# Counting argmax hits by sign masks on ScalarE for two of eight batches, in a gather and scatter kernel

## The chip, the cores and the metric

The kernel runs on one core of a Trainium2 chip. The metric is the device time of one execution in microseconds (us), lower is better. All runs quoted are with a granted TensorE clock of 1.0. TensorE, VectorE, ScalarE, GpSimd and SyncE appear in the profile as PE, DVE, ACT, POOL and SP; PEld is TensorE's weight load.

## The reference

```python
B, S, H = (8, 2048, 2560)          # scores [B,S,S], values [B,S,H], float32
best_j = np.argmax(scores, axis=2)
gathered = values[b_idx, best_j, :].copy()
out = np.zeros_like(values)
np.add.at(out, (b_idx, best_j, slice(None)), gathered)
```

A row j of a batch is thus written as `count[j] * values[j]`, where `count[j]` says how many rows of `scores` have their maximum in column j. About 37% of the counts are 0, 37% are 1 and 26% are higher.

## The kernel before

For each tile of 128 rows of scores, VectorE finds the maximum and then its column. After each four tiles, one-hot masks and a small matmul add up the counts:

```python
rows = room[:, place(x):place(x) + S]
nc.vector.max(out=mx[:], in_=rows)                                      # L196
nc.vector.max_index(out=am[:, g, :], in_max=mx[:], in_values=rows)      # L197
if g == G - 1:
    ...  # lo, hi, oh_lo, oh_hi on VectorE, then 4 matmuls into cnt_ps  # L200 to L212
```

`room` is one area of SBUF that holds the tiles of scores in a ring. The first two laps also use the places in which gathered rows will stand later (`NX` = 7 of them, besides `NB` = 14 permanent slots):

```python
def place(x):
    return NV * H + (x % turn - NX if x < 2 * turn else (x - 2 * turn) % NB) * S   # turn = NX + NB
```

When a batch is counted, GpSimd issues its output: rows with count 1 are copied from DRAM to DRAM (`copy_once`), rows with count 0 get zeros, and rows with higher counts are gathered into `room`, scaled on ScalarE and scattered. For batch 0 this part is:

```python
def gathers():
    for k in range(MCAP):                                   # MCAP = 5
        v = stage()
        gather(v, mi[:, k:k + 1])
        nc.scalar.activation(out=v, in_=v, func=Copy, bias=0.0, scale=mc[:, k:k + 1])   # L370, name of Copy cut short
        staged.append(v)
        ...
if b == 0:
    zeros(range(nz))                 # 7 transfers
    while tiles[0] < turn + NX:      # until all tiles in the gathers' places are read
        yield
    gathers()
...
for k in range(MCAP):
    scatter(staged[k], mi[:, k:k + 1], ...)
```

The order of the program is kept on TensorE, VectorE, ScalarE and SyncE. `yield` marks where the scan of the next batch's tiles goes on.

Of the kernel before, what the change touches and what calls it, by code (L numbers as in the profile page):

```python
# [8 lines left out]
FP32 = mybir.dt.float32  # L9
BF16 = mybir.dt.bfloat16  # L10
FP16 = mybir.dt.float16
INT32 = mybir.dt.int32
U32 = mybir.dt.uint32
ALU = mybir.AluOpType
P = 128
# [21 lines left out]
def kernel(  # L37
# [6 lines left out]
    nc = tc.nc  # L44
    B, S, S2 = scores.shape
    _, _, H = values.shape
    assert S == S2
    NT = S // P
    BIG = float(1 << 24)
    R = 4  # L50
    G = 4
    NV = 6
    NX = NV * H // S
    NB = 14
    NM = NT // 2
    NE = 16
    LE = P // NE
# [6 lines left out]
    out_flat = out.rearrange("b s h -> (b s) h")  # L64
    last_row = nc.gpsimd.to_reg(B * S - 1)

    consts = ctx.enter_context(tc.tile_pool(name="consts", bufs=1))
    small = ctx.enter_context(tc.tile_pool(name="small", bufs=3))
    fin = ctx.enter_context(tc.tile_pool(name="fin", bufs=2))
    ohp = ctx.enter_context(tc.tile_pool(name="ohp", bufs=1))  # L70
    lev = ctx.enter_context(tc.tile_pool(name="lev", bufs=1))
    psum_c = ctx.enter_context(tc.tile_pool(name="psum_c", bufs=2, space=bass.MemoryType.PSUM))
    psum_f = ctx.enter_context(tc.tile_pool(name="psum_f", bufs=1, space=bass.MemoryType.PSUM))
# [13 lines left out]
    row_f = consts.tile([P, NT], FP32)  # L87
# [3 lines left out]
    lane_f = consts.tile([P, P], FP32)  # L91
# [7 lines left out]
    ones = consts.tile([P, P], BF16)  # L99
# [15 lines left out]
    zero1 = consts.tile([P, 1], FP32)  # L115
    nc.vector.memset(zero1[:], 0.0)

    zrow = ctx.enter_context(nc.sbuf_tensor([P, H], FP32))
    nc.scalar.copy(zrow[:], zero1[:].to_broadcast([P, H]))


    room = ctx.enter_context(nc.sbuf_tensor([P, NV * H + NB * S], FP32))
    nc.scalar.copy(room[:, 0:NV * H - NX * S], zero1[:].to_broadcast([P, NV * H - NX * S]))
    turn = NX + NB
# [6 lines left out]
    loads, x = {}, 0  # L131
    while x < B * NT:
        n = 1
        most_n = 1 if x < 2 or 2 * turn - 6 <= x < 2 * turn else 2 if x < 4 or 2 * turn <= x < 4 * NT else R
        while n < most_n and (x + n) % NT and place(x + n) == place(x) + n * S:
            n += 1
        loads[x] = n
        x += n

    ones_i = ctx.enter_context(nc.sbuf_tensor([P, B * NT], INT32))  # L140
    zero_i = ctx.enter_context(nc.sbuf_tensor([P, B * NT], INT32))
    many_i = ctx.enter_context(nc.sbuf_tensor([P, B * NM], INT32))
    many_c = ctx.enter_context(nc.sbuf_tensor([P, B * NM], FP32))

# [5 lines left out]
    def after_waits(ins):  # L150
        tc.declare_no_dep(ins.ins, group="zrow", reason="GpSimd has waited for the transfers ahead of it")
# [12 lines left out]
    def gather(v, idx, note=lambda ins: None):  # L164
        note(nc.gpsimd.indirect_dma_start(  # L165
            out=v, out_offset=None, in_=values_flat[:, :],
            in_offset=bass.IndirectOffsetOnAxis(ap=idx, axis=0), bounds_check=B * S - 1, oob_is_err=False))
# [9 lines left out]
    def stage():  # L177
        v = room[:, vslot[0] * H:(vslot[0] + 1) * H]
        vslot[0] = (vslot[0] + 1) % NV
        return v  # L180

    def count_steps(b, cnt_ps):

        am = None
        for t in range(NT):
            x = b * NT + t
            if x in loads:
                n = loads[x]
                nc.sync.dma_start(out=room[:, place(x):place(x) + n * S],
                                  in_=scores[b, t * P:(t + n) * P, :].rearrange("(p r) s -> p (r s)", r=n))  # L190
            g = t % G
            if g == 0:
                am = small.tile([P, G, 8], U32, name="am")
            rows = room[:, place(x):place(x) + S]
            mx = small.tile([P, 8], FP32)
            nc.vector.max(out=mx[:], in_=rows)  # L196
            nc.vector.max_index(out=am[:, g, :], in_max=mx[:], in_values=rows)  # L197
            if g == G - 1:
                lo = small.tile([P, G], U32)
                nc.vector.tensor_single_scalar(out=lo[:], in_=am[:, :, 0], scalar=P - 1, op=ALU.bitwise_and)  # L200
                hi = small.tile([P, G], U32)
                nc.vector.tensor_single_scalar(out=hi[:], in_=am[:, :, 0], scalar=7, op=ALU.logical_shift_right)  # L202
                oh_lo = small.tile([P, G, P], BF16)
                nc.vector.tensor_tensor(  # L204
                    out=oh_lo[:], in0=lo[:].unsqueeze(2).to_broadcast([P, G, P]),
                    in1=lane_f[:].unsqueeze(1).to_broadcast([P, G, P]), op=ALU.is_equal)
                oh_hi = small.tile([P, G, NT], BF16)
                nc.vector.tensor_tensor(  # L208
                    out=oh_hi[:], in0=hi[:].unsqueeze(2).to_broadcast([P, G, NT]),
                    in1=lane_f[:, 0:NT].unsqueeze(1).to_broadcast([P, G, NT]), op=ALU.is_equal)  # L210
                for k in range(G):
                    nc.tensor.matmul(out=cnt_ps[:], lhsT=oh_lo[:, k, :], rhs=oh_hi[:, k, :],  # L212
                                     start=(t == G - 1 and k == 0), stop=(t == NT - 1 and k == G - 1))
            tiles[0] = x + 1
            yield

    def level_engines(rank):

# [59 lines left out]
    def value_steps(b, cnt_ps):  # L278

        cnt = fin.tile([P, NT], FP32)  # L280
# [23 lines left out]
        for c in range(2):  # L304
            nc.vector.tensor_tensor_scan(out=inc[:, c, :], data0=ones_f[:], data1=m[:, c, :], initial=0.0,
                                         op0=ALU.mult, op1=ALU.add)
# [15 lines left out]
        if b == B - 1:  # L322
            level_engines(rank[:, 0, :])
        hi = fin.tile([P, 2, NT], U32)
        nc.vector.tensor_copy(hi[:], rank[:])
        nc.vector.tensor_single_scalar(out=hi[:], in_=hi[:], scalar=7, op=ALU.logical_shift_right)
        lo = fin.tile([P, NT], U32)
# [4 lines left out]
            out=oh[:], in0=lo[:].unsqueeze(2).to_broadcast([P, NT, P]),  # L332
            in1=fill_f[:].unsqueeze(1).to_broadcast([P, NT, P]), op=ALU.is_equal)

        ez = fin.tile([P, NT, NT], FP16)
        nc.vector.tensor_tensor(  # L336
            out=ez[:], in0=hi[:, 0, :].unsqueeze(2).to_broadcast([P, NT, NT]),
            in1=lane_f[:, 0:NT].unsqueeze(1).to_broadcast([P, NT, NT]), op=ALU.is_equal)
        em = fin.tile([P, NT, NM], FP16)
        nc.vector.tensor_tensor(  # L340
            out=em[:], in0=hi[:, 1, :].unsqueeze(2).to_broadcast([P, NT, NM]),
            in1=lane_f[:, 0:NM].unsqueeze(1).to_broadcast([P, NT, NM]), op=ALU.is_equal)
        put = fin.tile([P, NT, 2 * NM + NT], FP16)
        nc.vector.tensor_tensor(out=put[:, :, 0:NM], in0=em[:], in1=row1_f[:].unsqueeze(2).to_broadcast([P, NT, NM]), op=ALU.mult)  # L344
        nc.vector.tensor_tensor(out=put[:, :, NM:2 * NM], in0=em[:], in1=cnt[:].unsqueeze(2).to_broadcast([P, NT, NM]), op=ALU.mult)
        nc.vector.tensor_tensor(out=put[:, :, 2 * NM:], in0=ez[:], in1=row1_f[:].unsqueeze(2).to_broadcast([P, NT, NT]), op=ALU.mult)  # L346
# [12 lines left out]
        for dst, x, n in ((zi, 2 * NM, NT), (mi, 0, NM)):  # L359
            nc.vector.scalar_tensor_tensor(out=dst, in0=e[:, x:x + n], scalar=float(b * S - 1), in1=l_ps[:, x:x + n],  # L360
                                           op0=ALU.add, op1=ALU.add)
# [40 lines left out]
    with tc.manual_schedule(engines={ET.PE, ET.DVE, ET.Activation, ET.SP}):  # L402
        pending = iter(())
        for b in range(B):
            cnt_ps = psum_c.tile([P, NT], FP32)
            for _ in count_steps(b, cnt_ps):
                next(pending, None)
            for _ in pending:
                pass
            pending = value_steps(b, cnt_ps)  # L410
            for _ in range((1, 4, 0)[min(b, 2)]):
                next(pending)
        for _ in pending:
            pass
        full = fin.tile([1, 2], FP32)
        nc.vector.tensor_reduce(out=full[:, 0:1], in_=tots[0:1, 0, 0:B - 1], op=ALU.max, axis=mybir.AxisListType.X)
        nc.vector.tensor_reduce(out=full[:, 1:2], in_=tots[0:1, 1, :], op=ALU.max, axis=mybir.AxisListType.X)
        over = fin.tile([1, 3], FP32)
        nc.vector.tensor_single_scalar(out=over[:, 0:1], in_=full[:, 0:1], scalar=float(ZCAP * P), op=ALU.is_gt)
        nc.vector.tensor_single_scalar(out=over[:, 1:2], in_=full[:, 1:2], scalar=float(MCAP * P), op=ALU.is_gt)  # L420
        nc.vector.tensor_single_scalar(out=over[:, 2:3], in_=most[0:1, :], scalar=float(ZLAST * LE), op=ALU.is_gt)
        over_i = fin.tile([1, 1], INT32)
        nc.vector.tensor_reduce(out=over_i[:], in_=over[:], op=ALU.max, axis=mybir.AxisListType.X)

    more = nc.values_load(over_i[0:1, 0:1], engines=[mybir.EngineType.Pool], min_val=0, max_val=2)
    spilt = tc.alloc_semaphore("spilt")
    with tc.If(more > 0):

# [3 lines left out]
        def one_by_one(ins):  # L432
            nonlocal n_spilt, last
            writes_out(ins)
            after_waits(ins)
            tc.add_to_no_dep_group("zrow", ins.ins)
            ins.then_inc(spilt, 16)
            tc.info.no_tile_sem_insts.add(ins.ins.name)
            n_spilt += 1
            with tc.issue_after(ins.ins):  # L440
                last = nc.gpsimd.wait_ge(spilt, 16 * n_spilt)
# [6 lines left out]
        for b in range(B):  # L448
            for k in range(MCAP, NM):
# [7 lines left out]
                with tc.issue_after(scaled.ins):  # L457
                    scatter(zrow[:], many_i[:, i:i + 1], one_by_one)

    last = nc.gpsimd.wait_ge(landed, 16 * n_free[0])  # L460
    with tc.issue_after(last.ins):
        nc.gpsimd.dma_reset()
# [30 lines left out]
```

## Time and profile before

| What | Before |
|---|---|
| Median of 4 runs beside the changed kernel | 828.87 us (827.58 to 828.96) |
| Span of the profiled run | 825.6 us |
| VectorE busy | 679.0 us, 82% |
| ScalarE busy | 101.2 us, 12% |
| Bytes moved by DMA | 347.04 MB, 420 GB/s |
| First transfer of output, batch 0 and batch 1 | 85.80 and 171.08 us |

The lines that carry this stand in the prediction. They are read so: each digit of a row is the busy share of one of 40 slices, in tenths. DMA is the mean over the 16 transfer engines. q1 is the queue of score loads, q0 the queue of everything that GpSimd issues.

### The profile page before, as it was taken

How to read it: one execution, taken by the hardware profiler on the slowest of the kernel's cores; microseconds unless marked ns; L12 is line 12 of the kernel's file. 1: busy time of each engine (PE TensorE's matmuls, PEld its weight loads, DVE VectorE, ACT ScalarE, POOL GpSimd, SP SyncE). 2: the span in 40 equal slices, each digit the busy share in tenths (PEclk: the TensorE clock that was granted, in tenths of full speed). 3: DMA queues.
4: the chain of work that ended last, by engine and by line, in shares of the span. 5: the costliest groups of instructions: out<-in, count | busy, mean ns of one | idle time of the engine just before them, and what ended most of it. 6: DMA issues, size and time to landing. Idle time of an engine off the chain costs nothing.

```text
span 825.6 us, 2045 instructions
## 1 busy us (share of the span) xinstructions
PE 14.7 (2%) x273; PEld 14.1 (2%) x273; DVE 679.0 (82%) x794; ACT 101.2 (12%) x43; POOL 274.7 (33%) x277
## 2 busy tenths in 40 slices
PE   0000000000000000000000000000000000000000
PEld 0000000000000000000000000000000000000000
DVE  7999999999999999999999999999999996000000
ACT  2000000500220002210002300013100320230230
POOL 0000651266121260152501343501505266346351
DMA  9999999999999999999999999999999999999997
GB/s 384 432 431 429 413 409 423 392 410 413 426 429 427 423 431 431 427 424 432 420 428 429 439 419 431 419 436 430 430 415 421 425 426 423 425 427 422 424 426 313
DMA packets 45664, 347.04 MB, mean 420 GB/s; under 512 B 18742, under 2 KB 18742, under 8 KB 18742
## 3 DMA queue, kind: packets, MB, share of 16 engines
q0 software_dynamic: 38736, 212.67, 62.1%
q1 hardware_dynamic: 6912, 134.22, 38.1%
q14 instruction: 14, 0.11, 0.0%
q8 instruction: 2, 0.03, 0.0%
HBM read 354.42 MB, written 300.15 MB: 793 GB/s over the span
## 4 chain that ended last, share of the span: by engine, by line
DVE 71%; DMA 13%; issue 8%; POOL 5%; another core or an unknown queue 1%; POOLq 0%; PE 0%; DVEq 0%
DVE am L197 32%; DVE mx L196 30%; DMA room<-in_values_dram,many_i 8%; DMA out_dram<-room,many_i 4%; POOL out_dram L33 2%; DVE oh_lo L204 2%; POOL out_dram L170 2%; DVE oh L331 2%; POOL room L165 1%; DMA room<-in_scores_dram 1%; DVE lo L200 1%; DVE oh_hi L208 0%; DVE hi L202 0%; DVE put L346 0%
## 5 line engine op out<-in xcount | busy, mean ns | idle before, releaser
L196 DVE MAX8 mx<-room 128x8 f32<-128x2048 f32 x128 | 291.7, 2279 | 4.6 <-DMA room<-in_scores_dram 4.6
L197 DVE FIND_INDEX8 am<-mx,room 128x8 uint32<-128x2048 f32 x128 | 292.4, 2285 | 0.0
L370 ACT ACTIVATE room<-room,many_c 128x2560 f32<-128x2560 f32 x40 | 96.7, 2426 | 693.0 <-DMA room<-in_values_dram,many_i 693.0
L33 POOL DMA_INDIRECT out_dram<-in_values_dram,ones_i x128 | 131.2, 1025 | 145.7 <-DVE m L302 107.7
L170 POOL DMA_INDIRECT out_dram<-room,many_i x40 | 39.7, 994 | 248.2 <-ACT room L370 248.2
L165 POOL DMA_INDIRECT room<-in_values_dram,many_i x40 | 41.8, 1046 | 122.2 <-DMA out_dram<-room,many_i 73.9
L170 POOL DMA_INDIRECT out_dram<-zrow,zero_i x61 | 60.8, 996 | 18.8 <-issue 18.8
L204 DVE TENSOR_TENSOR oh_lo<-lo,lane_f 128x512 bf16<-128x512 uint32 x32 | 22.1, 692 | 0.3
L331 DVE TENSOR_TENSOR oh<-lo,fill_f 128x2048 f16<-128x2048 uint32 x8 | 18.3, 2291 | 0.3
L212 PE MATMUL cnt_ps<-oh_hi,oh_lo 128*128 128x16 bf16 x128 | 8.1, 174 | 572.9 <-DVE oh_hi L208 528.7
L212 PEld LDWEIGHTS <-oh_lo 128*128 128x128 bf16 x128 | 8.4, 105 | 572.7 <-DVE oh_lo L204 547.3
L197 DVE MATCH_VALUE_LOAD am<-mx,room 128x8 f32 x128 | 11.8, 92 | 4.3
L208 DVE TENSOR_TENSOR oh_hi<-hi,lane_f 128x64 bf16<-128x64 uint32 x32 | 7.0, 218 | 0.0
L200 DVE TENSOR_SCALAR lo<-am 128x4 uint32<-128x4 uint32 x32 | 5.7, 178 | 1.1
L349 PE MATMUL l_ps<-put,oh 128*128 128x32 f16 x128 | 4.7, 188 | 73.4 <-DVE put L346 73.4
L349 PEld LDWEIGHTS <-oh 128*128 128x128 f16 x128 | 4.7, 104 | 74.5 <-DVE oh L331 64.1
L202 DVE TENSOR_SCALAR hi<-am 128x4 uint32<-128x4 uint32 x32 | 5.5, 172 | 0.0
L336 DVE TENSOR_TENSOR ez<-hi,lane_f 128x256 f16<-128x256 uint32 x8 | 3.3, 417 | 0.0
L346 DVE TENSOR_TENSOR put<-ez,row_f 128x256 f16<-128x256 f16 x8 | 3.3, 417 | 0.0
L321 DVE TENSOR_SCALAR rank<-base,off_ps 128x16 f32<-128x16 f32 x16 | 3.2, 244 | 0.0
L358 DVE TENSOR_SCALAR e<-l_ps 128x32 f32<-128x32 f32 x8 | 1.5, 184 | 2.0 <-PE l_ps L349 2.0
L344 DVE TENSOR_TENSOR put<-em,row_f 128x128 f16<-128x128 f16 x8 | 2.4, 298 | 0.3
(88 smaller groups left out, 53.5 us busy)
## 6 DMA issues: line engine op xcount, KB each, us to landing
room<-in_scores_dram SPq DMA_DIRECT2D x20, 4096.0 KB, 23.6
room<-in_scores_dram SPq DMA_DIRECT2D x18, 2048.0 KB, 11.7
room<-in_scores_dram SPq DMA_DIRECT2D x9, 1024.0 KB, 8.4
room<-in_scores_dram SPq DMA_DIRECT2D x1, 3072.0 KB
out_dram<-in_values_dram,ones_i POOLq DMA_INDIRECT x128
out_dram<-zrow,zero_i POOLq DMA_INDIRECT x61
room<-in_values_dram,many_i POOLq DMA_INDIRECT x40, 33.3
out_dram<-room,many_i POOLq DMA_INDIRECT x40, 51.4
```

The source lines that it names most:

```text
L33: return eng.add_instruction(ins)
L165: note(nc.gpsimd.indirect_dma_start(out=v, out_offset=None, in_=values_flat[:, :], in_offset=bass.IndirectOffsetOnAxis(ap=idx, axis=0), bo ...
L170: note(nc.gpsimd.indirect_dma_start(out=out_flat[:, :], out_offset=bass.IndirectOffsetOnAxis(ap=idx, axis=0), in_=v, in_offset=None, bound ...
L196: nc.vector.max(out=mx[:], in_=rows)
L197: nc.vector.max_index(out=am[:, g, :], in_max=mx[:], in_values=rows)
L200: nc.vector.tensor_single_scalar(out=lo[:], in_=am[:, :, 0], scalar=P - 1, op=ALU.bitwise_and)
L204: nc.vector.tensor_tensor(out=oh_lo[:], in0=lo[:].unsqueeze(2).to_broadcast([P, G, P]), in1=lane_f[:].unsqueeze(1).to_broadcast([P, G, P]) ...
L208: nc.vector.tensor_tensor(out=oh_hi[:], in0=hi[:].unsqueeze(2).to_broadcast([P, G, NT]), in1=lane_f[:, 0:NT].unsqueeze(1).to_broadcast([P, ...
L212: nc.tensor.matmul(out=cnt_ps[:], lhsT=oh_lo[:, k, :], rhs=oh_hi[:, k, :], start=(t == G - 1 and k == 0), stop=(t == NT - 1 and k == G - 1))
L331: nc.vector.tensor_tensor(out=oh[:], in0=lo[:].unsqueeze(2).to_broadcast([P, NT, P]), in1=fill_f[:].unsqueeze(1).to_broadcast([P, NT, P]), ...
L349: nc.tensor.matmul(out=l_ps[:], lhsT=oh[:, t, :], rhs=put[:, t, :], start=(t == 0), stop=(t == NT - 1))
L370: nc.scalar.activation(out=v, in_=v, func=mybir.ActivationFunctionType.Copy, bias=0.0, scale=mc[:, k:k + 1])
```

## The change

The intent is to take work off VectorE in the first two batches, so that their counts, and with them the output transfers, come sooner. Batches 0 and 1 no longer ask for the column of the maximum. ScalarE computes `Sign(max - score)`, which is 0 at the maximum and 1 elsewhere, and adds it up along the row. A row with a sole maximum has the sum S - 1. For each such row TensorE adds 1 to the counts of all columns and subtracts the row's mask, which leaves a 1 in the column of the maximum. If a row has ties, a branch at the end does both batches again. To make room, the ring loses one slot, and the sizes of the score loads are set anew.

```diff
-    NB = 14
+    NB = 13
+    FAST = 2
...
-        most_n = 1 if x < 2 or 2 * turn - 6 <= x < 2 * turn else 2 if x < 4 or 2 * turn <= x < 4 * NT else R
+        most_n = 1 if x < 2 or NT - 2 <= x < NT else 2 if x < 4 or NT - 4 <= x < NT or 2 * turn <= x < 3 * NT else R
...
+    def compare(rows):
+        mx = small.tile([P, 8], FP32, name="mx")
+        nc.vector.max(out=mx[:], in_=rows)
+        less = lessp.tile([P, S], BF16, name="less")
+        n_less = small.tile([P, 1], FP32, name="n_less")
+        nc.scalar.activation(out=less[:], in_=rows, func=mybir.ActivationFunctionType.Sign, bias=mx[:, 0:1], scale=-1.0,
+                             accum_out=n_less[:])
+        return less, n_less
+
+    def count_less(b, t, less, n_less, cnt_ps):
+        w = sole[:, b * NT + t:b * NT + t + 1]
+        nc.vector.tensor_scalar(out=w, in0=n_less[:], scalar1=float(S - 1), scalar2=-1.0, op0=ALU.is_equal, op1=ALU.mult)
+        nc.tensor.matmul(out=cnt_ps[:], lhsT=minus[:], rhs=w.to_broadcast([P, NT]), start=(t == 0), stop=False)
+        for c in range(NT):
+            nc.tensor.matmul(out=cnt_ps[:, c:c + 1], lhsT=less[:, c * P:(c + 1) * P], rhs=w, start=False, ...)
...
+            if b < FAST:
+                found = compare(rows)
+                if waiting is not None:
+                    count_less(b, t - 1, *waiting, cnt_ps)
+                waiting = found
...
-    more = nc.values_load(over_i[0:1, 0:1], engines=[mybir.EngineType.Pool], min_val=0, max_val=2)
+    more = nc.values_load(over_i[0:1, 0:1], engines=[ET.Pool, ET.DVE, ET.PE], min_val=0, max_val=2)
...  (cut: the tie check, the redo of both batches in the branch, three tiles moved to another pool)
```

More of the change, by code (lines that the diff above doesn't have):

```diff
@@ L70 @@
     ohp = ctx.enter_context(tc.tile_pool(name="ohp", bufs=1))
+    lessp = ctx.enter_context(tc.tile_pool(name="lessp", bufs=2))
     lev = ctx.enter_context(tc.tile_pool(name="lev", bufs=1))
@@ L116 @@
     nc.vector.memset(zero1[:], 0.0)
+    minus = consts.tile([P, P], BF16)
+    nc.vector.memset(minus[:], -1.0)
+    sole = consts.tile([P, FAST * NT], BF16)
     zrow = ctx.enter_context(nc.sbuf_tensor([P, H], FP32))
@@ L141 @@
     zero_i = ctx.enter_context(nc.sbuf_tensor([P, B * NT], INT32))
+    some_i = ctx.enter_context(nc.sbuf_tensor([P, FAST * NT], INT32))
     many_i = ctx.enter_context(nc.sbuf_tensor([P, B * NM], INT32))
@@ L180, in stage, with find_maxima, count_places @@
         return v
+    def find_maxima(rows, t, am):
+        g = t % G
+        if g == 0:
+            am = small.tile([P, G, 8], U32, name="am")
+        mx = small.tile([P, 8], FP32, name="mx")
+        nc.vector.max(out=mx[:], in_=rows)
+        nc.vector.max_index(out=am[:, g, :], in_max=mx[:], in_values=rows)
+        return am
+    def count_places(am, t, cnt_ps):
+        lo = small.tile([P, G], U32, name="lo")
+        nc.vector.tensor_single_scalar(out=lo[:], in_=am[:, :, 0], scalar=P - 1, op=ALU.bitwise_and)
+        hi = small.tile([P, G], U32, name="hi")
+        nc.vector.tensor_single_scalar(out=hi[:], in_=am[:, :, 0], scalar=7, op=ALU.logical_shift_right)
+        oh_lo = small.tile([P, G, P], BF16, name="oh_lo")
+        nc.vector.tensor_tensor(
+            out=oh_lo[:], in0=lo[:].unsqueeze(2).to_broadcast([P, G, P]),
+            in1=lane_f[:].unsqueeze(1).to_broadcast([P, G, P]), op=ALU.is_equal)
+        oh_hi = small.tile([P, G, NT], BF16, name="oh_hi")
+        nc.vector.tensor_tensor(
+            out=oh_hi[:], in0=hi[:].unsqueeze(2).to_broadcast([P, G, NT]),
+            in1=lane_f[:, 0:NT].unsqueeze(1).to_broadcast([P, G, NT]), op=ALU.is_equal)
+        for k in range(G):
+            nc.tensor.matmul(out=cnt_ps[:], lhsT=oh_lo[:, k, :], rhs=oh_hi[:, k, :],
+                             start=(t == G - 1 and k == 0), stop=(t == NT - 1 and k == G - 1))
@@ new lines, in compare @@
+    def compare(rows):
+        mx = small.tile([P, 8], FP32, name="mx")
+        nc.vector.max(out=mx[:], in_=rows)
+        less = lessp.tile([P, S], BF16, name="less")
[8 more added lines that the diff above has]
+        for c in range(NT):
+            nc.tensor.matmul(out=cnt_ps[:, c:c + 1], lhsT=less[:, c * P:(c + 1) * P], rhs=w, start=False, stop=(t == NT - 1 and c == NT - 1))
@@ L182, in count_steps @@
     def count_steps(b, cnt_ps):
-        am = None
+        am, waiting = None, None
         for t in range(NT):
@@ L190, in count_steps @@
                                   in_=scores[b, t * P:(t + n) * P, :].rearrange("(p r) s -> p (r s)", r=n))
-            g = t % G
-            if g == 0:
-                am = small.tile([P, G, 8], U32, name="am")
             rows = room[:, place(x):place(x) + S]
-            mx = small.tile([P, 8], FP32)
-            nc.vector.max(out=mx[:], in_=rows)
-            nc.vector.max_index(out=am[:, g, :], in_max=mx[:], in_values=rows)
-            if g == G - 1:
-                lo = small.tile([P, G], U32)
-                nc.vector.tensor_single_scalar(out=lo[:], in_=am[:, :, 0], scalar=P - 1, op=ALU.bitwise_and)
-                hi = small.tile([P, G], U32)
-                nc.vector.tensor_single_scalar(out=hi[:], in_=am[:, :, 0], scalar=7, op=ALU.logical_shift_right)
-                oh_lo = small.tile([P, G, P], BF16)
-                nc.vector.tensor_tensor(
-                    out=oh_lo[:], in0=lo[:].unsqueeze(2).to_broadcast([P, G, P]),
-                    in1=lane_f[:].unsqueeze(1).to_broadcast([P, G, P]), op=ALU.is_equal)
-                oh_hi = small.tile([P, G, NT], BF16)
-                nc.vector.tensor_tensor(
-                    out=oh_hi[:], in0=hi[:].unsqueeze(2).to_broadcast([P, G, NT]),
-                    in1=lane_f[:, 0:NT].unsqueeze(1).to_broadcast([P, G, NT]), op=ALU.is_equal)
-                for k in range(G):
-                    nc.tensor.matmul(out=cnt_ps[:], lhsT=oh_lo[:, k, :], rhs=oh_hi[:, k, :],
-                                     start=(t == G - 1 and k == 0), stop=(t == NT - 1 and k == G - 1))
+            if b < FAST:
[3 more added lines that the diff above has]
+                waiting = found
+            else:
+                am = find_maxima(rows, t, am)
+                if t % G == G - 1:
+                    count_places(am, t, cnt_ps)
             tiles[0] = x + 1
             yield
+        if waiting is not None:
+            count_less(b, NT - 1, *waiting, cnt_ps)
     def level_engines(rank):
@@ L333, in value_steps @@
             in1=fill_f[:].unsqueeze(1).to_broadcast([P, NT, P]), op=ALU.is_equal)
-        ez = fin.tile([P, NT, NT], FP16)
+        ez = ohp.tile([P, NT, NT], FP16)
         nc.vector.tensor_tensor(
@@ L338, in value_steps @@
             in1=lane_f[:, 0:NT].unsqueeze(1).to_broadcast([P, NT, NT]), op=ALU.is_equal)
-        em = fin.tile([P, NT, NM], FP16)
+        em = ohp.tile([P, NT, NM], FP16)
         nc.vector.tensor_tensor(
@@ L342, in value_steps @@
             in1=lane_f[:, 0:NM].unsqueeze(1).to_broadcast([P, NT, NM]), op=ALU.is_equal)
-        put = fin.tile([P, NT, 2 * NM + NT], FP16)
+        put = ohp.tile([P, NT, 2 * NM + NT], FP16)
         nc.vector.tensor_tensor(out=put[:, :, 0:NM], in0=em[:], in1=row1_f[:].unsqueeze(2).to_broadcast([P, NT, NM]), op=ALU.mult)
@@ L417 @@
         nc.vector.tensor_reduce(out=full[:, 1:2], in_=tots[0:1, 1, :], op=ALU.max, axis=mybir.AxisListType.X)
-        over = fin.tile([1, 3], FP32)
+        worst = fin.tile([P, 1], BF16)
+        nc.vector.tensor_reduce(out=worst[:], in_=sole[:], op=ALU.max, axis=mybir.AxisListType.X)
+        sole_ps = psum_f.tile([P, 1], FP32)
+        nc.tensor.matmul(out=sole_ps[:], lhsT=ones[:], rhs=worst[:], start=True, stop=True)
+        over = fin.tile([1, 4], FP32)
+        nc.vector.tensor_single_scalar(out=over[:, 3:4], in_=sole_ps[0:1, :], scalar=-float(P), op=ALU.is_gt)
         nc.vector.tensor_single_scalar(out=over[:, 0:1], in_=full[:, 0:1], scalar=float(ZCAP * P), op=ALU.is_gt)
@@ L458 @@
                     scatter(zrow[:], many_i[:, i:i + 1], one_by_one)
+        for b in range(FAST):
+            cnt_ps = psum_c.tile([P, NT], FP32)
+            am = None
+            for t in range(NT):
+                rows = room[:, 0:S]
+                with tc.issue_after(last.ins):
+                    after_waits(nc.gpsimd.dma_start(out=rows, in_=scores[b, t * P:(t + 1) * P, :]))
+                am = find_maxima(rows, t, am)
+                if t % G == G - 1:
+                    count_places(am, t, cnt_ps)
+            cnt = fin.tile([P, NT], FP32)
+            nc.vector.tensor_copy(cnt[:], cnt_ps[:])
+            some_f = fin.tile([P, NT], FP32)
+            nc.vector.tensor_scalar(out=some_f[:], in0=cnt[:], scalar1=0.0, scalar2=BIG, op0=ALU.is_equal, op1=ALU.mult)
+            nc.vector.scalar_tensor_tensor(out=some_f[:], in0=some_f[:], scalar=float(b * S), in1=row_f[:], op0=ALU.add, op1=ALU.add)
+            nc.vector.tensor_copy(some_i[:, b * NT:(b + 1) * NT], some_f[:])
+            for t in range(NT):
+                with tc.issue_after(last.ins):
+                    empty = nc.gpsimd.memset(zrow[:], 0.0)
+                after_waits(empty)
+                with tc.issue_after(empty.ins):
+                    gather(zrow[:], some_i[:, b * NT + t:b * NT + t + 1], one_by_one)
+                with tc.issue_after(last.ins):
+                    scaled = nc.gpsimd.tensor_scalar(out=zrow[:], in0=zrow[:], scalar1=cnt[:, t:t + 1], scalar2=None, op0=ALU.mult)
+                after_waits(scaled)
+                with tc.issue_after(scaled.ins):
+                    one_by_one(nc.gpsimd.dma_start(out=out_flat[b * S + t * P:b * S + (t + 1) * P, :], in_=zrow[:]))
     last = nc.gpsimd.wait_ge(landed, 16 * n_free[0])
```

## The prediction

> **What bounds the kernel now.** I read the page from its second part downwards: first the slices, then the queues, then the windows of 20 us, then the timeline round the first batch and at the end. The chain of waits names VectorE (71% of the span), and its two scans of the scores, MAX8 and FIND_INDEX8, fill 584 us. That is the tempting answer. The slices say otherwise:
>
> ```profile
> DVE  7999999999999999999999999999999996000000
> DMA  9999999999999999999999999999999999999997
> GB/s 384 432 431 429 413 409 423 392 410 413 426 429 427 423 431 431 427 424 432 420 428 429 439 419 431 419 436 430 430 415 421 425 426 423 425 427 422 424 426 313
> DMA packets 45664, 347.04 MB, mean 420 GB/s; under 512 B 18742, under 2 KB 18742, under 8 KB 18742
> ```
>
> VectorE is full for 33 of 40 slices and then stops, some 130 us before the end. The 16 DMA engines are full in every slice but the last, and the rate is the same (422 to 427 GB/s) after VectorE stopped. The two queues give the balance:
>
> ```profile
> q0 software_dynamic: 38736, 212.67, 62.1%
> q1 hardware_dynamic: 6912, 134.22, 38.1%
> ```
>
> Columns: packets, MB, share of 16 engines' span. q1 loads the scores. q0 carries everything that GpSimd issues: one-count rows copied from DRAM to DRAM, zero rows, and gathers and scatters of rows with higher counts. The shares add to 100.2% of 825.6 us: transfer engines have no hole. The transfer bound is therefore 827 us of packet time at today's rates, and only two things could lower it: fewer bytes or a better rate.
>
> How much better? Loads alone ran at 428 GB/s (20 to 80 us), q0 alone at 424 to 426 (700 to 800 us). The low stretches are these (window, then its length, busy time of the engines, clock, DMA share, GB/s):
>
> ```profile
> 0.00:20.00 20.00, 0.00 (x0) 0.00 (x0) 14.54 (x23) 4.55 (x3) 1.09 (x8) 1.00 0.96 393
> ...
> 140.00:160.00 20.00, 0.25 (x4) 0.26 (x4) 19.83 (x17) 7.28 (x3) 4.10 (x5) 1.00 0.97 409
> 160.00:180.00 20.00, 1.05 (x22) 0.97 (x22) 18.15 (x40) 4.75 (x2) 10.16 (x9) 1.00 1.00 400
> 180.00:200.00 20.00, 0.25 (x4) 0.26 (x4) 19.79 (x18) 0.00 (x0) 15.12 (x16) 1.00 1.01 401
> ...
> 820.00:826.00 6.00, 0.00 (x0) 0.00 (x0) 0.00 (x0) 0.00 (x0) 0.00 (x0) 1.00 0.22 75
> ```
>
> From 80 to 200 us the six windows average 409 GB/s (416, 404, 422, 409, 400, 401). At 426 the same bytes need 120 x 409/426 = 115.2 us, so 4.8 us are to be had there. The start loses 20 x (1 - 393/426) = 1.5 us. The end (820 to 826) costs some 5 us for landing and the closing wait.
>
> **What the Trainium skill says.** "DMA: Bandwidth & Descriptors", Specifications, gives a fabric ceiling of 435 GB/s for the 16 engines; the trace's 420 mean is 97% of it, which supports the reading of a full DMA. (The same table has 358 GB/s as a core's HBM limit; this trace runs above it throughout, so the measurement decides.) The same page, Issuing engines are not separate DMA queues, says that transfers from all engines share those 16 and interleave; the trace agrees, as q0 and q1 at 50.6% and 50.8% share 200 to 240 us. "ScalarE: Activation LUTs", Rules for kernel authors and the part on ACT_TABLE_LOAD, gives about 280 ns plus 0.833 ns per element with a per-partition bias operand: 2413 ns for 2560 columns against 2426 measured here for the scaling copy, so 1986 ns for 2048 columns is a safe estimate for the new Sign.
>
> **The change, part by part.**
>
> (1) Removed on VectorE: 32 FIND_INDEX8 at 2.285 us and their value loads at 0.092 (76.1 us), and in 8 groups lo 0.178, hi 0.172, oh_lo 0.692 and oh_hi 0.218 (10.1 us): 86 us. Added: 32 one-column operations, about 0.14 us each as the CAST of one column took (4.5 us). Net 82 us of VectorE work gone, all in batches 0 and 1. None lies on a path that sets the end, because the DMA is full beside it.
>
> (2) Added on ScalarE: 32 Sign of about 2.0 us (64 us) beside MAX8 at 2.28 us, so it keeps pace. ScalarE was 12% busy.
>
> (3) Added on TensorE: 17 small matmuls a tile. The 16 of L349 took 0.59 us as a run, so some 0.65 us a tile, beside a 2.4 us tile: free.
>
> (4) Batch 0's counts come sooner. Before, the first copy is issued at 85.80 us. After, VectorE takes about 2.45 us a tile, the same as a 1 MB tile takes to arrive at 428 GB/s (2.45 us). From the first landing at 5.65 us and the loads of four tiles at once I get tiles 8 to 11 landed at 32.5, tile 15 scanned at 52, its Sign and counts at 55, and the first copy at about 56 us: 30 us sooner. This fills no hole, since loads filled the engines until then; it changes the order of the same bytes.
>
> (5) Batch 1 gains little, and this is the step I trust least. Batch 0's five gathers are placed in the program when tile 26 has been compared, and their scaling copies stand in ScalarE's order **ahead of the Signs of tiles 27 to 31**. The gathers queue in q0 behind 16 copies and 7 zero writes (7.75 + 7.7 MB, from 37% of 16384 rows each, less the zeros beyond the seventh). Before, this took from 85.8 to 160 us. After, with q1 also busy, q0 gets 200 to 240 GB/s: 15.4 MB plus 5.3 MB of gathers take about 94 us, from 56 to 150. So ScalarE stands still from about 88 to 130 or 150, VectorE behind it once its three mx buffers are used, and batch 1's counts come at 155 to 168 us, against 170 before. From batch 2 on the work is as before.
>
> (6) The ring loses one slot (20 places instead of 21, 13 instead of 14 later). q1 loads up to tile 40 before it must wait for tile 27. From 21.6 tiles at 56 us, at 5.1 us a tile, that is reached at 150 us, about when ScalarE is free again. A hole is possible but short, and batch 0's scatters (5.3 MB, 13 us) lie there.
>
> (7) The check at the end: one reduction, one matmul, one comparison (under 1 us) on VectorE, which finishes over 100 us early; and a branch on three engines instead of one, in time in which GpSimd still waits for transfers. Hidden. Continuous random scores make ties so rare that the branch isn't taken.
>
> Sum: bytes unchanged, 347 MB. Up to 4.8 us from 80 to 200 us, of which I count half, as step 5 makes a stretch of the same kind: 828.9 - 2.4 gives 826.5. Better mixing of both queues (mixed stretches reach 437) may give another 1 us: **825.5 us**.
>
> **The rivals.**
>
> A: VectorE really is the bound, as the chain says. Then 82 us less would show nearly in full: 750 us. Against it: 130 us of q0 work remain after VectorE stops, and 347 MB at 435 GB/s need 798 us. Even a perfect DMA gives no more than 798 + 8 for start and end = 806.
>
> B: the wait of step 5 opens a hole: q1's ring is full while q0 has run dry, and the DMA stands for 10 to 20 us, for instance from 130 to 165 us. Then 838 to 848 us. For it: before, at 140 to 180 us, the rate already dips. Against it: by bytes q0 stays filled until 150.
>
> C: earlier writes mix with loads for longer and raise the rate by 1 to 2%: 812 to 820 us. For it: 540 to 560 us at 437. Against it: the mixed windows from 80 to 120 us have 416 and 404.
>
> **Range and chances.** The DMA bound makes a gain of over 2% (under 812.4 us) need 347 MB at more than 431 GB/s with start and end as they are: 0.04. A loss of over 2% (over 845.5 us) needs a hole of some 17 us: 0.05. The range 817 to 836 spans C's lesser half to B's lesser half.
>
> **What will show it.** VectorE busy falls from 679 to about 597 us, while the DMA row stays at 9 and MB at 347. The first copy is issued at 52 to 60 us. ScalarE shows a wait of 40 us or more on the gathered rows in the midst of batch 1's Signs, and VectorE's MAX8 shows a wait behind Sign. Batch 1's first copy comes at 155 to 172 us instead of 171.08. The prediction is wrong if slices between 100 and 180 us fall below 8 on the DMA row (B), if the mean rate rises over 431 GB/s (C), or if Sign takes over 2.4 us, so that ScalarE sets the pace.

## The result

The changed kernel took 836.1 us (median of 4, 835.26 to 837.83) beside 828.87 us before. The ratio is 1.0094, with a 95% interval of 1.0074 to 1.0113: slower by 0.9%. Ratios here are the mean time of one kernel's fast runs over that of the other's of the same rounds, so they are not quite the ratio of the medians. The result is correct. The time lies just above the stated range.

The page of the changed kernel, whose span is 833.5 us, has these rows of 40 slices and these queues:

```profile
DVE  5886610179999999999999999999999995000000
ACT  6663600822300003200004100023000320230230
...
GB/s 387 430 431 429 430 373 428 383 339 425 432 430 426 425 424 440 426 420 431 425 431 431 426 427 419 424 430 421 429 425 412 422 427 414 425 426 420 424 425 266
...
q0 software_dynamic: 38736, 212.67, 61.8%
q1 hardware_dynamic: 6192, 134.22, 37.8%
```

VectorE now idles from about 106 to 163 us. Then it is as full as before and stops at about the same slice as before. The transfer rate falls in slices 8 and 9 (about 146 to 188 us) and in the last. It is low in slice 6 too (373 GB/s, 409 before), but there the engines are busy (share 1.00 from 100 to 120 us), and a run below that loses nothing has 359 there. The bytes are the same. The queues' shares add to 99.6% of 833.5 us, where before they added to 100.2% of 825.6 us. As a time this is 830.2 us of packets instead of 827.2, and 3.3 us of hole instead of an overlap of 1.6.

Where the stand-still comes from is plain in ScalarE's timeline of the changed kernel. The columns are start, duration, engine and line, operation, tiles, sizes, count, and in brackets the idle time ahead of it with what ended it:

```profile
101.81 2.00 ACT L222 ACTIVATE less<-room,mx 128x2048 bf16<-128x2048 f32 x1 [0.21 <-DVE sole L229]
...
146.85 2.43 ACT L411 ACTIVATE room<-room,many_c 128x2560 f32<-128x2560 f32 x1 [42.95 <-DMA room<-in_values_dram,many_i]
149.91 2.43 ACT L411 ACTIVATE room<-room,many_c 128x2560 f32<-128x2560 f32 x1 [0.63 <-DMA room<-in_values_dram,many_i]
152.96 2.43 ACT L411 ACTIVATE room<-room,many_c 128x2560 f32<-128x2560 f32 x1 [0.63 <-DMA room<-in_values_dram,many_i]
156.05 4.75 ACT L411 ACTIVATE room<-room,many_c 128x2560 f32<-128x2560 f32 x2 [0.66 <-DMA room<-in_values_dram,many_i]
160.70 1.99 ACT L222 ACTIVATE less<-room,mx 128x2048 bf16<-128x2048 f32 x1
```

L222 is the Sign and L411 is batch 0's scaling copy. Each Sign is followed by a short instruction that reads its row sum, which is left out here. The Sign at 101.81 is that of tile 26. The next Sign waits 57 us, until five scaling copies are done, and the first of these waits 43 us for its gathered rows. Before, the same wait for the first rows was harmless, because ScalarE had nothing else to do:

```profile
151.14 2.43 ACT L370 ACTIVATE room<-room,many_c 128x2560 f32<-128x2560 f32 x1 [145.84 <-DMA room<-in_values_dram,many_i]
```

VectorE's waits show the stand-still from the other side (who waits, for whom, total us, times, longest us). SyncE's timeline shows what follows for the loads (SPq is its sequencer, each line one or more loads issued):

```profile
DVE sole L229 <- ACT less L222: 75.6, 6, 56.5
```

```profile
75.35 0.33 SPq L241 DMA_DIRECT2D room<-in_scores_dram  x1
```

```profile
164.79 5.20 SPq L241 DMA_DIRECT2D room<-in_scores_dram  x2
```

No score load was issued from 75.35 to 164.79 us: the ring was full. The next load is of two tiles, 40 and 41, and needs the places of tiles 27 and 28, whose Signs started at 160.70 and 162.69 us; the second ended at 164.68. Meanwhile GpSimd's queue ran dry too. These two lines from GpSimd's timeline of the changed kernel are the last scatter of batch 0 and the first copy of batch 1:

```profile
161.07 0.97 POOL L177 DMA_INDIRECT out_dram<-room,many_i  x1 [1.35 <-ACT room L411]
173.93 0.98 POOL L33 DMA_INDIRECT out_dram<-in_values_dram,ones_i  x1 [11.90 <-DVE m L343]
```

Batch 1's first copy came at 173.93 us, later than the 171.08 of before, although 79 us of VectorE's busy time had been saved. The windows of the changed kernel from 140 us on have the hole (last two columns: DMA share, GB/s):

```profile
140.00:160.00 20.00, 0.00 (x0) 0.00 (x0) 0.00 (x0) 11.24 (x5) 3.92 (x4) 1.00 0.96 405
160.00:180.00 20.00, 3.56 (x102) 3.25 (x101) 13.54 (x33) 11.05 (x11) 6.12 (x5) 1.00 0.95 365
180.00:200.00 20.00, 0.21 (x8) 0.10 (x4) 19.21 (x18) 2.43 (x1) 15.42 (x16) 1.00 0.95 374
```

From 160 to 200 us the share adds to 20 x (0.95 + 0.95) = 38.0 us, against 20 x (1.00 + 1.01) = 40.2 before. The end grew as well. From 800 us to the end of the span, time minus packet time is 4.7 us before (shares 0.98 for 20 us and 0.24 for 5.6) and 7.0 us after (1.01 for 20 us and 0.47 for 13.5).

### The profile page after: what moved, and what is told of

Read it like the earlier page. It is cut to its first block, busy times and chain, and to the rows that moved or that the text cites. A ratio compares the mean times of both kernels' runs of the same rounds, so it can differ in the third digit from the quotient of the medians.

```text
span 833.5 us, 3112 instructions
## 1 busy us (share of the span) xinstructions
PE 31.8 (4%) x786; PEld 29.2 (4%) x786; DVE 600.4 (72%) x733; ACT 167.9 (20%) x107; POOL 276.2 (33%) x277
## 4 chain that ended last, share of the span: by engine, by line
DVE 41%; issue 16%; DMA 15%; another core or an unknown queue 11%; POOL 10%; ACT 4%; PE 0%; POOLq 0%; SPq 0%; ACTq 0%; DVEq 0%
DVE am L196 16%; DVE mx L195 15%; DMA room<-in_values_dram,many_i 8%; POOL out_dram L33 5%; DMA out_dram<-room,many_i 4%; DVE mx L219 4%; DMA room<-in_scores_dram 4%; POOL out_dram L177 3%; ACT less L222 2%; POOL room L172 2%; DVE oh L372 1%; ACT room L411 1%; DVE oh_lo L205 1%; DVE lo L201 0%
## 5 line engine op out<-in xcount | busy, mean ns | idle before, releaser
L196 DVE FIND_INDEX8 am<-mx,room 128x8 uint32<-128x2048 f32 x96 | 219.4, 2285 | 0.0
L411 ACT ACTIVATE room<-room,many_c 128x2560 f32<-128x2560 f32 x40 | 96.6, 2428 | 590.0 <-DMA room<-in_values_dram,many_i 590.0
L33 POOL DMA_INDIRECT out_dram<-in_values_dram,ones_i x128 | 133.4, 1042 | 141.2 <-DVE m L343 103.1
L222 ACT ACTIVATE less<-room,mx 128x2048 bf16<-128x2048 f32 x32 | 64.0, 2001 | 43.0 <-DVE sole L229 17.6
L229 DVE TENSOR_SCALAR sole<-n_less 128x1 bf16<-128x1 f32 x32 | 4.8, 150 | 75.9 <-ACT less L222 75.6
L232 PEld LDWEIGHTS <-less 128*128 128x128 bf16 x512 | 16.2, 104 | 143.3 <-ACT less L222 119.1
L232 PE MATMUL cnt_ps<-sole,less 128*128 128x1 bf16 x512 | 18.2, 165 | 0.0
L205 DVE TENSOR_TENSOR oh_lo<-lo,lane_f 128x512 bf16<-128x512 uint32 x24 | 16.6, 693 | 0.3
L196 DVE MATCH_VALUE_LOAD am<-mx,room 128x8 f32 x96 | 8.8, 92 | 3.3
L230 PE MATMUL cnt_ps<-sole,minus 128*128 128x16 bf16 x32 | 5.5, 172 | 144.1 <-DVE sole L229 131.7
L222 ACT ACTIVATION_READ_ACCUMULATOR less<-room,mx 128x1 f32 x32 | 6.0, 187 | 0.0
```

What stands on the lines that cost most here:

```text
L33: return eng.add_instruction(ins)
L205: nc.vector.tensor_tensor(out=oh_lo[:], in0=lo[:].unsqueeze(2).to_broadcast([P, G, P]), in1=lane_f[:].unsqueeze(1).to_broadcast([P, G, P]) ...
L222: nc.scalar.activation(out=less[:], in_=rows, func=mybir.ActivationFunctionType.Sign, bias=mx[:, 0:1], scale=-1.0, accum_out=n_less[:])
L232: nc.tensor.matmul(out=cnt_ps[:, c:c + 1], lhsT=less[:, c * P:(c + 1) * P], rhs=w, start=False, stop=(t == NT - 1 and c == NT - 1))
L411: nc.scalar.activation(out=v, in_=v, func=mybir.ActivationFunctionType.Copy, bias=0.0, scale=mc[:, k:k + 1])
```

## The experiments

Three theories were put up. **Stall**: ScalarE's order, with batch 0's scaling copies ahead of the Signs of tiles 27 to 31, freezes scans and loads until both transfer queues are dry. **Ring**: one slot less and other load sizes cost the time. **Redo**: the tie check, the branch on three engines and the longer tail cost it.

### The scaling copies moved behind the Signs

```diff
                 gather(v, mi[:, k:k + 1])
-                nc.scalar.activation(out=v, in_=v, func=Copy, bias=0.0, scale=mc[:, k:k + 1])
                 staged.append(v)
+                if b > 0:
+                    scale(k)
...
             gathers()
+            while tiles[0] < FAST * NT:
+                yield
+            for k in range(MCAP):
+                scale(k)
```

> Batch 0's gathers are issued where they were, but their five scaling copies on ScalarE stand behind the Signs of tiles 27 to 31 instead of ahead of them. Stall theory (ScalarE waits 43 us for the gathered rows and freezes batch 1's scans and the score loads behind it): the 56 us wait of the one-column operation on Sign vanishes, batch 1's counts are ready by 120 us, the transfer hole at 160 to 190 us goes, time 826 to 830 us. Ring theory (one slot less and other load sizes cost the time): 834 to 838 us as after. Redo theory (the branch on three engines and the longer tail): 834 to 838 us.

It took 827.96 us, ratio 1.0003 (0.9987 to 1.0020). VectorE's 56.5 us wait is gone, and the longest on that line is now 9.0:

```profile
DVE sole L229 <- ACT less L222: 19.1, 5, 9.0
```

The windows of this run where the hole had been:

```profile
160.00:180.00 20.00, 0.25 (x4) 0.26 (x4) 19.83 (x17) 2.43 (x1) 0.00 (x0) 1.00 0.99 424
180.00:200.00 20.00, 0.26 (x4) 0.27 (x4) 19.83 (x17) 9.10 (x4) 3.91 (x4) 1.00 0.98 398
```

The Sign of batch 1's last tile starts at 113 us, and loads resume at 108 us. The stall theory holds. With the changed ring, loads, check and branch all left in, neither of the others can carry the loss by itself. Whether 14 slots would have outlasted the stall was not tested, so the smaller ring may have a part in the loss.

The time at which the output comes is not what was repaired. In this run batch 1's first copy is issued at 202.16 us, 28 us later than in the changed kernel, because in GpSimd's order it stands behind batch 0's scatters, and those wait for the late scaling copies. Nothing is lost by it, as the loads flow.

### The ring and the load sizes alone, in the kernel before

```diff
-    NB = 14
+    NB = 13
...
-        most_n = 1 if x < 2 or 2 * turn - 6 <= x < 2 * turn else 2 if x < 4 or 2 * turn <= x < 4 * NT else R
+        most_n = 1 if x < 2 or NT - 2 <= x < NT else 2 if x < 4 or NT - 4 <= x < NT or 2 * turn <= x < 3 * NT else R
```

> The kernel before with 13 slots and the new load sizes alone, counts as before. Stall theory: 827 to 830 us, as before. Ring theory: 833 to 838 us. Redo theory: 827 to 830 us.

It took 837.39 us, ratio 1.0115 (1.0096 to 1.0135). Alone, this part of the change costs as much as the whole change, just as the ring theory had said; the 827 to 830 us of the stall theory were missed. But it does so by another hole, at 80 to 100 us, which the changed kernel doesn't have (1.01 and 431 GB/s there):

```profile
80.00:100.00 20.00, 1.03 (x22) 0.97 (x22) 19.13 (x38) 0.00 (x0) 11.48 (x10) 1.00 0.80 320
```

With the old counting, loads must bridge the time to 85.8 us alone, since no output transfer exists before. One slot less, and the ring is full too soon. So the earlier counts do have a worth: they let the ring be smaller. A part that costs 1.2% alone costs nothing that can be measured in the presence of another (the run before this one), and taking the parts' costs as a sum would have misled.

### The slot alone, and the load sizes alone

```diff
-    NB = 14
+    NB = 13
```

> The kernel before with one slot less, its own load sizes kept (single tiles at the end of the second lap of the ring). If the missing slot made the ring-only run slow: 834 to 838 us. If the load of four tiles at that place did: 828 to 831 us.

```diff
-        most_n = 1 if x < 2 or 2 * turn - 6 <= x < 2 * turn else 2 if x < 4 or 2 * turn <= x < 4 * NT else R
+        most_n = 1 if x < 2 or NT - 2 <= x < NT else 2 if x < 4 or NT - 4 <= x < NT or 2 * turn <= x < 3 * NT else R
```

> The kernel before with all 14 slots and the new load sizes. If the missing slot made the ring-only run slow: 827 to 830 us. If the load of four tiles late in the second lap did: 832 to 838 us, with that load issued some 20 us later than the first of the single ones was.

The slot alone took 833.31 us (1.0059, 1.0042 to 1.0076) and the load sizes alone took 833.4 us (1.0055, 1.0029 to 1.0082). Neither of my alternatives was right: each carries about half. With one slot less, the share falls to 0.64 from 80 to 90 us (1.00 before):

```profile
80.00:90.00 10.00, 0.45 (x6) 0.39 (x6) 9.34 (x22) 0.00 (x0) 3.27 (x4) 1.00 0.64 246
```

With the load sizes alone, the same place is at 0.94 for 20 us:

```profile
80.00:100.00 20.00, 1.03 (x22) 0.97 (x22) 19.13 (x38) 0.00 (x0) 11.54 (x10) 1.00 0.94 369
```

The old sizes had single tiles at the end of the second lap, issued at 83.2, 91.2, 100.6 and 105.7 us as places came free. The new ones have one load of four tiles there, which waits for the last of its four places and is issued at 105.6 us.

### The new count in batch 0 alone

```diff
-    FAST = 2
+    FAST = 1
```

> The changed kernel with the new count in batch 0 alone; all Signs are then issued before the first gather, so nothing can stall behind it; ring, loads, check and branch stay as in the change. Stall theory: 826 to 831 us. Ring theory and redo theory: 834 to 838 us.

It took 828.94 us, ratio 1.0020 (0.9997 to 1.0042). With no Sign left behind the gathers there is nothing to stall, and the loss is gone within the error. Ring, loads, check and branch are in this run too.

### The new count in batches 0, 1 and 2

```diff
-    FAST = 2
+    FAST = 3
```

> The changed kernel with the new count in batches 0, 1 and 2; batch 1's scaling copies then stand ahead of all of batch 2's Signs, a second stall of the same kind. Stall theory: a second hole at 180 to 240 us, time 839 to 860 us. Ring theory and redo theory: 834 to 839 us, as after; a pure gain of VectorE time would give less than 836.

It took 835.3 us, ratio 1.0096 (1.0079 to 1.0113): a miss for my expectation. The second stall is there, as VectorE's row is at 0 or 4 tenths from 188 to 229 us, but the DMA has no second hole:

```profile
200.00:220.00 20.00, 1.19 (x34) 1.07 (x34) 4.61 (x4) 11.14 (x7) 13.63 (x14) 1.00 1.02 423
```

This second stall of ScalarE and VectorE cost nothing that shows, and GpSimd's queue held work through it. In the first stall that queue runs dry, in the second it doesn't: from 188 to 229 us it takes 85.9% of the engines' time, and the rate is 422 GB/s. This mends the stall theory: the loss is the time in which *both* queues are short, and not the wait itself.

### The wait made shorter, the order left

```diff
         if b == 0:
-            zeros(range(nz))
-
             while tiles[0] < turn + NX:
                 yield
             gathers()
+            zeros(range(nz))
```

> The changed kernel with batch 0's seven zero writes queued after its gathers, so that the gathers stand behind 16 transfers and not 23. ScalarE's order is untouched. Stall theory: the scaling copies start about 20 us sooner (120 to 130 us instead of 147), score loads resume about 20 us sooner than 164.8 us, time 827 to 832 us. If the order of ScalarE itself and not the length of the wait mattered: 835 to 838 us.

It took 828.38 us, ratio 1.0001 (0.9984 to 1.0018). ScalarE still stands 34.65 us, but its first scaling copy starts at 129.52 instead of 146.85 us, loads resume at 147.4 instead of 164.8, and seven zero transfers are left to fill the time:

```profile
160.00:180.00 20.00, 0.59 (x16) 0.58 (x16) 18.78 (x22) 0.00 (x0) 10.74 (x10) 1.00 1.01 425
180.00:200.00 20.00, 0.26 (x4) 0.27 (x4) 19.83 (x17) 0.00 (x0) 9.76 (x10) 1.00 1.01 423
```

Here the stall survives and the loss doesn't, as the mended theory has it. The edit does two things at once, a shorter wait and work left in the queue for the time after it; the run doesn't part them. It is also the only run of these with both new batches in which batch 1's output comes clearly sooner than before (first copy at 156.59 us, 171.08 before), and that gained nothing.

### No redo

The tie check, the redo and the branch on VectorE and TensorE were taken out. The data has no ties, so the result stays right.

```diff
-    more = nc.values_load(over_i[0:1, 0:1], engines=[ET.Pool, ET.DVE, ET.PE], min_val=0, max_val=2)
+    more = nc.values_load(over_i[0:1, 0:1], engines=[ET.Pool], min_val=0, max_val=2)
...  (the tie check ahead of it and "for b in range(FAST): ..." inside the branch removed)
```

> The changed kernel without the tie check, the redo and the branch on VectorE and TensorE (the data has no ties, so the result stays right). Stall theory: 834 to 837 us, unchanged. Redo theory: 826 to 831 us.

It took 836.5 us, ratio 1.0096 (1.0079 to 1.0113), as with the redo. That theory is out.

### Both repairs

The two edits, scaling copies behind the Signs and zeros behind the gathers, in one kernel.

> The changed kernel with both repairs: scaling copies behind the Signs of tiles 27 to 31, and the seven zero writes behind the gathers. If a full transfer queue is the bound, nothing is left to gain: 826 to 829 us, ratio to before 0.997 to 1.001. If VectorE's saved time still had a use, less than 824 us.

It took 827.48 us in 5 runs (826.78 to 828.05), beside 828.59 us, ratio 0.9987 (0.9974 to 1.0001). It has the lowest ratio of the runs, but is not shown to be faster than the kernel before. Even with the hole closed and 80 us of VectorE work saved, at most 0.3% can have been gained.

## Why the prediction was wrong

**The bound (part one, and rival A): right.** VectorE's busy time fell by 79 us (679.0 to 600.4) and the time didn't fall. With both repairs it is the same as before within the error. (A small slip: VectorE's row before has 32 full slices, not 33.) The better rate of rival C did not come either: the mean is 416 GB/s after, and 420 or 421 in the repaired kernels.

**Steps 1 to 4: right.** Sign took 2.00 us (about 1.99 by the Trainium skill, "ScalarE: Activation LUTs", What ACT_TABLE_LOAD costs). The first copy was predicted at 56 us and came at 55.43.

**Step 5: right in mechanism and nearly so in size.** The scaling copies were to stand ahead of the Signs of tiles 27 to 31 and hold ScalarE from about 88 to 130 or 150 us; it was held from 104 to 146.85. Batch 1's first copy was to come at 155 to 172 us and came at 173.93. I had let the Signs resume at 150, but they resume after the fifth scaling copy, at 160.70.

**Step 6 failed.** "A hole is possible but short, and batch 0's scatters (5.3 MB, 13 us) lie there." The sum then gave a gain of 2.4 us in the stretch from 80 to 200 us. In its place, the packet time from 0 to 200 us is 2.8 us less than before (20 us times the shares of ten windows: 196.4 against 199.2), and the total is 7.2 us worse. In bytes the loss is larger. From 100 to 200 us (`--windows 100:200`) the rate was 407 GB/s before and 389 after, and 413 in the run that moves the scaling copies alone. Against that run the changed kernel falls 2.4 MB behind there, which is 5.6 us at 425 GB/s, and its profiled span is 6.9 us longer. Two things were wrong in the step:

- The scatters do not fill the hole. The fifth is issued at 161.07 us, and the next transfers in that queue at 173.93, when five Signs, the counts and VectorE's operations on them are done. Rival B had described this hole, "from 130 to 165 us", and made it 838 to 848 us; it came later and the total was 836.1. The sign set down for it, slices below 8 on the DMA row, did not appear: the row stays at 9, as the share was 0.95. The row of GB/s shows the hole (383 and 339).
- The two queues do not share by bytes, as I had assumed when I gave q0 "200 to 240 GB/s". From 56 to 100 us in the changed kernel (packets, MB, share):

```profile
q1 hardware_dynamic: 587, 17.14, 90.4%
q0 software_dynamic: 535, 1.81, 10.2%
```

In this stretch both queues hold work. The packets are about one for one, the bytes nine to one: loads of four tiles come in packets of 32 KB, while q0's copies are of 10 KB, and most of its packets are skipped rows of a few bytes. The Trainium skill, "DMA: Bandwidth & Descriptors", Queues, rings and completion order, says that each engine takes turns between queues packet by packet; these counts agree, if its packet, which may hold many descriptors, is the profile's, which no run here shows. So the last load that fitted was issued at 75.35 us, and not near the 150 us of my estimate, and q0 had the engines alone from 108 to 160 us. The bytes ahead of the gathers were the same in either order. I take this to be why the wrong share did not spoil the timing of step 5; that its time came out was luck to this extent.

**Step 7: right.** Without the redo the time is the same.

**What stays open.** The hole of 2.8 us until 200 us is not the whole 7.2 us. The tail grew by 2.3 us, and the sum of packet times by 3.0 us (827.2 to 830.2), though the bytes are the same. The longer tail does not belong to the stall alone: from 800 us to the end, time minus packet time is 6.2 to 6.7 us in the three repaired kernels too (shares 0.76, 0.75 and 0.75 of 26.6, 26.8 and 25.0 us), and they lose nothing. They are ahead of the kernel before at 200 us (417, 416 and 421 GB/s from the start, 413 before) and lose that lead in the tail; why is not shown. The longer packet times are open as well. The ring-only run has them (99.3% of 836.8 us is 830.9 us of packets, for a loss of 9.5 us), the first two repairs don't (826.6 and 826.8 us), and the slot-only run hardly does (99.6% of 831.7 us is 828.4), though it loses 0.6%. A hole may hit some of the 16 engines harder than others, and the span ends with the last one. The trace has no engine number for a packet, so this is argued and not shown.

## What to carry to other kernels

Where transfers fill the span, ask of a change first whether some queue will always hold work: here 79 us saved on an engine off that path were worth nothing, and a stall cost nothing that was measured until the last queue ran dry. Before work is given to an engine that keeps program order, look at what it already waits for: a copy that waited for a transfer harmlessly becomes a barrier for everything placed behind it. A buffer count and a load size tuned for one schedule must be tested against the other one; here they cost 1.2% in the old schedule and nothing measurable in the repaired new one.

## What the Trainium skill lacked or had wrong

- "DMA: Bandwidth & Descriptors", Queues, rings and completion order: it has the turns by packet, but not the consequence that the byte share follows the packet size. Here 587 packets against 535 moved 17.14 MB against 1.81 MB, which suggests that the size of the loads set how long the other queue got little; no run here changed that size alone in this stretch.
- The same page, Specifications: the row with about 358 GB/s as a core's limit to HBM stands without its condition. The page's part on bandwidth gives that figure for both cores of a pair streaming, and 425 GB/s for one core alone. So the 420 GB/s that this one-core kernel moved over 825.6 us does not contradict the page, though the prediction took it so.
- "ScalarE: Activation LUTs", What ACT_TABLE_LOAD costs: its figure for an ACTIVATE with a bias operand (1.99 us for 2048 columns) fits the 2.00 us measured, but a Sign with a row sum is followed by a second instruction, ACTIVATION_READ_ACCUMULATOR, of 0.187 us each in 32 of 32 cases, which that section doesn't count.
